# Second-layer attention with four score banks, one projection bank, and odd softmax chunks scaled by POOL

## The chip, the core and the metric

The kernel runs on one core of one Trainium2 chip. The metric is the device time of one execution in microseconds, lower is better; the time before is the median of three runs. A core has five engines that run beside each other and wait for one another by semaphores: PE (TensorE: matmuls and transposes), DVE (VectorE), ACT (ScalarE), POOL (GpSimd) and SP (SyncE, which here only issues DMAs). Matmul results land in PSUM, of which there are eight banks of 128 partitions x 512 f32; PE writes them, ACT and DVE read them, POOL does not touch them here.

## The reference, cut to what matters

The program is a two-layer decoder trunk on 512 tokens of width 1024. Layer 0 is a gated DeltaNet layer, layer 1 a sliding-window attention with grouped heads; each layer also attends with four heads into 256 memory tokens, and each ends with an output projection and a SwiGLU block. The change is in the attention of layer 1:

```python
proj = h @ swa_w_q[bl]                       # 512 x 1024: 768 window queries, 256 memory queries
q = apply_partial_rope(proj[..., :768], cos, sin)
# window attention, 12 heads of 64, per block of 128 queries over 256 keys (previous and own block)
s = einsum(q, k) * (64 ** -0.5); s = where(mask, s, -inf)
m = maximum(max(s), sink)
p = exp(s - m)
p = p / (sum(p) + exp(sink - m))
o = einsum(p, v)
# memory attention, 4 heads of 64, over 256 memory tokens
s = einsum(mem_q, mem_k) * (64 ** -0.5); o = einsum(softmax(s), mem_v)
x = x + concat([mix_out, mem_o]) @ w_out[layer]
x = x + swiglu(rms_norm(x), w_gate_up, w_down)
```

## The kernel before, in words

Activations lie transposed: a tile holds 128 features (partitions) x 512 tokens. Every large product is done in three f32r matmuls per 128x128 weight block (`mm3`: high part by high part, high by low, low by high), so a projection of one 128-feature tile (`project`) is 8 blocks x 3 = 24 matmuls of 128x512 that accumulate in one PSUM bank. The weight of a projection is loaded by SP into `wraw`, its high part made by ACT (`whi`), its low part by DVE (`wlo`).

The attention of layer 1 is `swa`. It has eight query tiles: 0 to 5 are window tiles (two heads each), 6 and 7 memory tiles. `queries(t)` projects one tile; for a window tile `rope` then reads the bank twice on DVE (a stream shuffle, a multiply by `cosT`), multiplies by `sinT` and adds. `score(t)` makes the scores of the four token chunks n = 0 to 3 and both heads b: the PSUM tile `qk` is two banks and holds two chunks, so a tile takes two of them. For window tiles DVE adds the band mask and takes the maximum (one custom instruction and one accumulator read per chunk and head) into `sm` in SBUF; for memory tiles DVE takes the maximum and ACT writes the exponentials. `weigh(t)` then does the rest: ACT takes the exponentials of a window tile, DVE the reciprocal of the sums, each chunk is scaled in place (even n by DVE with `ts`, odd n by ACT with `copy`), PE transposes it into a `pt` bank, the transposed chunk is copied to `pf` (n = 2 by DVE, the others by ACT), and PE multiplies by the values into the bank `sc`, which `split` writes out as the pair `mix[t]` (ACT the high part `h`, DVE the low part `l`).

The eight banks of this stage are named in `build`: two for projections (`pj`), one for small things (`g`), one two-bank `qk` tile, two `pt`, one `sc`. The main loop, for t = 0 to 5, traces `queries(t + 1)`, `score(t)` and then `weigh` of the tile scored two steps earlier; the last two `weigh` follow the loop. `output` projects the eight mixed tiles to x with banks pj, pj, g in turn; it takes the mixed tiles in the order 6, 7, 0 to 5, so that it can begin before the last are there.

The order of the work on each engine is not the order of the text: a scheduler with costs of its own places the traced instructions on each engine ahead of time, and on the chip each engine works its list strictly in that order and stops where a semaphore is missing. PE therefore fills its waits with matmuls of the next projection only where the list has them.

Of the kernel before, what the change touches and what calls it, by code (L numbers as in the profile page):

```python
# [13 lines left out]
ALU = mybir.AluOpType  # L14
# [4 lines left out]
P = 128  # L19
# [4 lines left out]
NC = 4  # L24
# [61 lines left out]
class Builder:  # L86
# [139 lines left out]
    def build(self):  # L226
        tc, nc, a = self.tc, self.nc, self.a
        with ExitStack() as st:
            opened = lambda name, **kw: tc.tile_pool(name=name, bufs=1, reuse_waits="tile", **kw)
            pool = lambda name, **kw: st.enter_context(opened(name, **kw))  # L230
            cp = pool("const")
            self.wpool, self.apool = pool("w"), pool("acta")
            self.dpool = pool("scratch", space=DRAM)
            self.load_constants(cp)
            self.weng = nc.vector
            with opened("layer0", side="right") as self.mpool:
                with self.banks(pj=3, g=2, sc=3):
                    with opened("early", side="right") as ep:
                        self.mem_and_norm(ep)
                        self.gates(ep)  # L240
                    with opened("gdn", side="right") as gp:
                        mix = self.gdn(gp)
                    self.bpool, xp = pool("actb"), pool("x")
                    self.x = [self.t(xp, [P, T], F32, f"x{k}") for k in range(KD)]
                    for k in range(KD):
                        nc.sync.dma_start(self.x[k], a["xT"][:, k, :])
                    self.rstd, self.cosT, self.sinT = (self.t(xp, [P, T], F32, n) for n in ("rstd", "cosT", "sinT"))
                    h = self.output(xp, 0, mix, self.bpool)
            with opened("ffn0", side="right") as fp, self.banks(pj=2, g=6):
                self.ffn(fp, xp, 0, h, self.apool, rope=True)  # L250
            with self.banks(pj=2, g=1, qk=1, pt=2, sc=1):
                with opened("swa", side="right") as sp:
                    mix = self.swa(sp)
                h = self.output(xp, 1, mix, self.apool)
            with opened("ffn1", side="right") as fp, self.banks(pj=2, g=6):
                self.ffn(fp, xp, 1, h, self.bpool)
# [492 lines left out]
        return sm, mx, den, nm  # L749

    def weigh(self, pool, scores, vv, m, out, sinks):

        nc = self.nc
        win = sinks is not None
        own = "pt" in self.pbufs
        half = [slice(0, 64), slice(64, P)]
        sm, mx, den, nm = scores
        if win:
            sk = sinks.unsqueeze(2).to_broadcast([P, 2, NC])
            v4 = lambda ap: ap.rearrange("p (b n) -> p b n", b=2)  # L760
            self.stt(v4(mx), v4(mx), 0.125, sk, ALU.mult, ALU.max)
            self.ts(nm, mx, -1.0, ALU.mult)
            es = self.t(pool, [P, 2 * NC], F32, "es", 2)
            self.tt(nc.vector, v4(es), v4(nm), sk, ALU.add)
            self.fn(es, es, AF.Exp)
            for n in range(NC):
                c0 = 0 if n else P
                for b in range(2):
                    i = b * NC + n
                    self.fn(sm[n][:, b, c0:], sm[n][:, b, c0:], AF.Exp, scale=0.125, bias=nm[:, i:i + 1],  # L770
                            accum_out=den[:, i:i + 1])
            self.tt(nc.vector, den, den, es, ALU.add)
        nc.vector.reciprocal(den, den)
        o = self.bank("sc")
        group = NC if own else 2
        for n in range(NC):
            if n % group == 0:
                pf = {}
            k0 = 1 if win and n == 0 else 0
            p = sm[n][:, :, k0 * P:]  # L780
            dn = den.rearrange("p (b n) -> p n b", b=2)[:, n, :]
            for b in range(2):
                if n % 2:
                    self.copy(p[:, b], p[:, b], scale=dn[:, b:b + 1])
                else:
                    self.ts(p[:, b], p[:, b], dn[:, b:b + 1], ALU.mult)
            pt = self.bank("pt" if own else "g", [P, 2, 2, P])
            for j in range(k0, 2):
                for b in range(2):
                    turned = self.tr(pt[:, j, b, :], sm[n][:, b, j * P:(j + 1) * P])  # L790
                    if self.ahead is not None:

                        self.nosync(turned, self.ahead)
                        self.ahead = None
            pf[n] = self.t(pool, [P, 2, 2, P], F32, "pf", group)
            if own and n == 2:
                nc.vector.tensor_copy(pf[n][:, k0:], pt[:, k0:])
            else:
                self.copy(pf[n][:, k0:], pt[:, k0:])
            if (n + 1) % group:  # L800
                continue
            for n, t in pf.items():
                for j in range(1 if win and n == 0 else 0, 2):
                    for b in range(2):
                        v = vv[n - 1 + j][:, half[b]] if win else vv[j][:, m * P + 64 * b:m * P + 64 * b + 64]
                        ins = self.mm(o[half[b], n * P:(n + 1) * P], v, t[:, j, b, :], win and n == 0 or j == 0, j == 1)
                        if turned is not None:
                            self.nosync(ins, turned)
                            turned = None
        self.split(o, *out)  # L810


    def output(self, xp, layer, mix, hpool):

        nc, a = self.nc, self.a
        self.weng = nc.vector
        h = []
        self.acc = None
        for m in range(KD):
            ps = self.project(a["wout"][layer, m], mix, ("pj", "pj", "g")[m % 3],  # L820
                              (6, 7, 0, 1, 2, 3, 4, 5))
            self.tt(nc.vector, self.x[m], ps, self.x[m], ALU.add)
            hl = self.pair(hpool)
            self.split_gain(self.x[m], self.gain(G_FFN[layer], m), *hl)
            h.append(hl)
            self.acc = self.accumulate(xp, self.acc, self.x[m], m)
        return h
# [189 lines left out]

    def rstd_from(self, acc, t=slice(0, T)):
        self.use(LN_EXP)
        ps = self.bank("g")[:, t]  # L1020
        self.mm(ps, self.ones, acc)
        self.rsqrt(self.rstd[:, t], ps, D)

# [46 lines left out]
    def swa(self, sp):  # L1070
        nc, a = self.nc, self.a
        memK, memV = self.fetch(sp, "mk"), self.fetch(sp, "mv")
        hk, h, qs, mix = [], [], {}, {}
# [5 lines left out]
        kk, vv = [], []  # L1079

        def queries(t):
            ps = self.project(a["wq"][t], h)
            if len(qs) == 0:
                self.rstd_from(self.acc)
                for table in (self.cosT, self.sinT):
                    self.tt(nc.vector, table, table, self.rstd, ALU.mult)
            qs[t] = self.t(sp, [P, T], F32, "q", 3)
            if t < 6:
                self.rope(sp, ps, qs[t])
            else:  # L1090
                self.tt(nc.vector, qs[t], ps, self.rstd, ALU.mult)

        def keys():
            kk.append(self.t(sp, [P, T], F32, "ks"))
            self.rope(sp, self.project(a["wkv"][0], hk), kk[0])

        def values():
            ps = self.project(a["wkv"][1], hk)
# [3 lines left out]

        def transpose_values():
            v = vv.pop()
            pt = self.bank("g")
            for c in range(NC):
                self.tr(pt[:, c * P:(c + 1) * P], v[:, c * P:(c + 1) * P])
            vt = self.t(sp, [P, NC, P], F32, "vt")
            self.copy(vt.rearrange("p c i -> p (c i)"), pt)
            vv.extend(vt[:, c, :] for c in range(NC))  # L1110

        def score(t):
            got[t] = self.scores(sp, qs[t], kk[0] if t < 6 else memK[t - 6], t < 6)

        def weigh(t):
            mix[t] = self.pair(self.bpool)
            if t < 6:
                self.weigh(sp, got[t], vv, t, mix[t], sinks[:, t, :])
            else:
                self.weigh(sp, got[t], memV, t - 6, mix[t], None)  # L1120

        got = {}
        queries(6)
# [4 lines left out]
        transpose_values()  # L1128
        queries(0)
        score(7)  # L1130

        behind = [6, 7]
        for t in range(6):
            if t < 5:
                queries(t + 1)
            score(t)
            behind.append(t)
            weigh(behind.pop(0))
        for t in behind:
            weigh(t)  # L1140
        return [mix[t] for t in range(KD)]

    def final(self, fp, squares, t):
# [85 lines left out]
```

## Time and profile before

| | |
|---|---|
| time, median of 3 runs | 1168.39 us (1166.91 to 1168.46) |
| the profiled execution's own time | 1169.1 us |
| its span, first to last instruction | 1167.3 us |
| mean granted TensorE clock | 0.996 of full speed |
| busy: PE / weight loads / DVE / ACT / POOL | 1144.1 / 999.2 / 834.2 / 629.4 / 82.9 us |
| waits of PE over the whole span, longest first | 6.9, 2.2, 2.1, 1.0, 0.9, 0.9, 0.5, 0.4 us |

A page of the profile shows one execution: busy time by engine, the chain that ended last, and groups of equal instructions. The trace behind it gives every instruction with its start, its length and what ended the idle time before it. Rows of a timeline start with the start in us from the beginning of the span and the length in us; matmuls overlap, so the distance from start to start, not the length, is what one costs PE. In this execution `swa` runs from about 657 to 776 us, and the part from the first scores to the end of the second output projection from 682.4 to 778.1 us.

### The profile page before, as it was taken

Reading aid. Unit: us, or ns where it says so; the run is one execution under the profiler, and the core shown is the slowest. Engines: PE = TensorE matmul, PEld = TensorE weight load, DVE = VectorE, ACT = ScalarE, POOL = GpSimd, SP = SyncE. Lnnn points to the kernel's source line nnn. Section 1 sums busy time; section 2 is a strip of 40 time slices with the busy share of each in tenths; the row PEclk is TensorE's granted clock in tenths of the full one; section 3 lists DMA queues with packets and bytes.
Section 4 is the critical chain, followed back from the end, with each engine's and each line's share of the span. In section 5 each row is a group of like instructions: output and inputs, shape, how many; then the busy total and the mean of one; then the engine's idle time right before and its main releaser. Section 6 shows DMA issues by size and latency. Waiting matters only on the chain.

```text
span 1167.3 us, 19448 instructions
## 1 busy us (share of the span) xinstructions
PE 1144.1 (98%) x7410; PEld 999.2 (86%) x7410; DVE 834.2 (71%) x1558; ACT 629.4 (54%) x1250; POOL 82.9 (7%) x93
## 2 busy tenths in 40 slices
PE   7999999999999999999999999999999999999996
PEld 6888777877889998899998877688999988999986
DVE  6654877767788876488965768758788734889654
ACT  7579564366466642256643546865566422566433
POOL 0210000000011101011100000010011000111000
PEclk9999999999999999999999999999999999999998
DMA  8334352224557735467623421153477633776232
GB/s 306 126 110 113 114 127 92 72 91 162 163 136 187 175 102 155 123 165 180 163 79 99 129 82 55 37 126 110 100 189 183 155 99 106 168 171 172 76 99 84
DMA packets 72944, 151.22 MB, mean 130 GB/s; under 512 B 16732, under 2 KB 19444, under 8 KB 72852
## 3 DMA queue, kind: packets, MB, share of 16 engines
q1 hardware_dynamic: 61908, 130.06, 36.3%
q0 software_dynamic: 10944, 19.93, 10.9%
q8 instruction: 58, 0.95, 0.4%
q14 instruction: 34, 0.28, 0.1%
HBM read 143.00 MB, written 6.96 MB: 128 GB/s over the span
## 4 chain that ended last, share of the span: by engine, by line
PE 91%; ACT 4%; DVE 3%; DMA 1%; issue 0%; SPq 0%; DVEq 0%; ACTq 0%
PE pj L143 44%; PE g L143 39%; PE sc L143 6%; ACT sm L131 1%; PE g L147 1%; PE pt L147 1%; DVE wlo L150 1%; ACT sm L137 1%; DMA wraw<-in_wmk 1%; ACT whi L137 0%; ACT T L137 0%; PE qk L143 0%; DVE mx L743 0%; DVE sm L739 0%; DMA wraw<-in_wdn 0%
## 5 line engine op out<-in xcount | busy, mean ns | idle before, releaser
L137 ACT ACTIVATE whi<-wraw 128x512 fp32r<-128x512 f32 (+3 forms) x325 | 243.1, 754 | 292.3 <-PE pj L143 191.4
L150 DVE TENSOR_TENSOR wlo<-wraw,whi 128x512 fp32r<-128x512 f32 (+3 forms) x325 | 271.9, 845 | 109.0 <-ACT whi L137 103.5
L143 PE MATMUL pj<-h,whi 128*128 128x512 f32 (+1 forms) x676 | 265.9, 394 | 0.2
L143 PE MATMUL pj<-l,whi 128*128 128x512 f32 (+1 forms) x676 | 265.2, 392 | 0.0
L143 PE MATMUL pj<-h,wlo 128*128 128x512 f32 (+1 forms) x676 | 264.4, 392 | 0.0
L143 PE MATMUL g<-T,whi 128*128 128x256 f32 x1216 | 220.5, 282 | 0.0
L143 PEld LDWEIGHTS g<-T,whi 128*128 128x128 f32 x1216 | 187.0, 189 | 1.1 <-DVE fu L153 1.1
L143 PE MATMUL g<-T,wlo 128*128 128x256 f32 x608 | 171.1, 281 | 0.0
L143 PE MATMUL g<-h,whi 128*128 128x256 f32 (+1 forms) x516 | 152.8, 296 | 0.0
L143 PE MATMUL g<-h,wlo 128*128 128x256 f32 (+1 forms) x516 | 152.0, 295 | 0.0
L143 PE MATMUL g<-l,whi 128*128 128x256 f32 (+1 forms) x516 | 151.8, 294 | 0.0
L143 PEld LDWEIGHTS pj<-h,whi 128*128 128x128 f32 x676 | 127.1, 188 | 28.4 <-issue 2.7
L143 PEld LDWEIGHTS pj<-h,wlo 128*128 128x128 f32 x676 | 127.2, 188 | 27.2 <-issue 2.2
L143 PEld LDWEIGHTS pj<-l,whi 128*128 128x128 f32 x676 | 127.2, 188 | 26.3 <-issue 1.2
L143 PEld LDWEIGHTS g<-T,wlo 128*128 128x128 f32 x608 | 114.4, 188 | 0.0
L143 PEld LDWEIGHTS g<-h,whi 128*128 128x128 f32 x516 | 98.0, 190 | 2.9 <-issue 0.2
L143 PEld LDWEIGHTS g<-l,whi 128*128 128x128 f32 x516 | 97.9, 190 | 2.9 <-issue 0.5
L143 PEld LDWEIGHTS g<-h,wlo 128*128 128x128 f32 x516 | 98.0, 190 | 2.4
L978 POOL DMA_DIRECT2D ws<-in_wgu x38 | 33.6, 883 | 735.1 <-DVE wlo L150 335.3
L137 ACT ACTIVATE whi<-ws 128x512 fp32r<-128x512 f32 x76 | 48.0, 631 | 49.3 <-PE g L143 41.2
L150 DVE TENSOR_TENSOR fu<-pj,rstd 128x512 f32<-128x512 f32 (+1 forms) x34 | 22.4, 660 | 53.0 <-PE pj L143 53.0
L150 DVE TENSOR_TENSOR wlo<-ws,whi 128x512 fp32r<-128x512 f32 x76 | 52.1, 686 | 7.3 <-ACT whi L137 7.2
(346 smaller groups left out, 1626.0 us busy)
## 6 DMA issues: line engine op xcount, KB each, us to landing
wraw<-in_wgu SPq DMA_DIRECT2D x50, 512.0 KB, 4.1
ws<-in_wgu SPq DMA_DIRECT2D x76, 256.0 KB, 3.5
ws<-in_wgu POOLq DMA_DIRECT2D x76, 256.0 KB, 4.9
wraw<-in_win SPq DMA_DIRECT2D x26, 512.0 KB, 3.6
wraw<-in_wdn SPq DMA_DIRECT2D x32, 384.0 KB, 3.2
wraw<-in_wdn SPq DMA_DIRECT2D x32, 320.0 KB, 2.9
wraw<-in_wgu SPq DMA_DIRECT2D x38, 256.0 KB, 4.6
wraw<-in_wout SPq DMA_DIRECT2D x16, 512.0 KB, 3.6
```

Of the source, the lines that this page charges most:

```text
L131: ins = self.nc.scalar.activation(out, in_, func, **kw).ins
L137: self.copied = self.nc.scalar.activation(out, in_, AF.Copy, **kw).ins
L143: return self.nc.tensor.matmul(out, lhsT, rhs, start=start, stop=stop, skip_group_check=more).ins
L147: return self.nc.tensor.transpose(out, in_, self.ident[:k, :k]).ins
L150: return eng.tensor_tensor(out=out, in0=a, in1=b, op=op).ins
L978: nc.gpsimd.dma_start(s1, a22, accum_op=ALU.add)
```

## The change

The score tiles get two buffers of two banks (`qk=2`), and the projections one bank (`pj=1`); the bank `g` is gone from this stage. What used `g`, and the projections of query tile 7 and of the keys, use the `pt` banks, which are not needed for transposes yet at that time; the output projection takes pj, pt, pt in turn. `weigh` is cut in two functions, `softmax` (exponentials, reciprocal, all four scalings) and `weighed` (transposes and values), and the loop of `swa` traces `softmax` of a tile right after `weighed` of the one before it, that is one step earlier than before. The odd chunks are scaled by POOL in this stage (`tensor_scalar`), the even ones by DVE as before. `weigh` of layer 0 now calls both functions, so that its four scalings are traced ahead of its transposes; there the odd chunks stay on ACT.

On PE's list the two halves of a tile's scores now follow each other, and a projection is cut in at most three pieces: after the scores and the first transposes one matmul, after the first half of the values one to three, and then the rest.

```diff
-            with self.banks(pj=2, g=1, qk=1, pt=2, sc=1):
+            with self.banks(pj=1, qk=2, pt=2, sc=1):
...
     def weigh(self, pool, scores, vv, m, out, sinks):
+        self.softmax(pool, scores, sinks)
+        self.weighed(pool, scores, vv, m, out, sinks is not None)
+
+    def softmax(self, pool, scores, sinks):
...
         nc.vector.reciprocal(den, den)
+        for n in range(NC):
+            p = sm[n][:, :, P if win and n == 0 else 0:]
+            dn = den.rearrange("p (b n) -> p n b", b=2)[:, n, :]
+            for b in range(2):
+                if n % 2 and "pt" in self.pbufs:
+                    nc.gpsimd.tensor_scalar(out=p[:, b], in0=p[:, b], scalar1=dn[:, b:b + 1], scalar2=None, op0=ALU.mult)
+                elif n % 2:
+                    self.copy(p[:, b], p[:, b], scale=dn[:, b:b + 1])
+                else:
+                    self.ts(p[:, b], p[:, b], dn[:, b:b + 1], ALU.mult)
+
+    def weighed(self, pool, scores, vv, m, out, win):
...
-            for b in range(2):
-                if n % 2:
-                    self.copy(p[:, b], p[:, b], scale=dn[:, b:b + 1])
-                else:
-                    self.ts(p[:, b], p[:, b], dn[:, b:b + 1], ALU.mult)
             pt = self.bank("pt" if own else "g", [P, 2, 2, P])
...
-            ps = self.project(a["wout"][layer, m], mix, ("pj", "pj", "g")[m % 3],
+            ps = self.project(a["wout"][layer, m], mix, ("pj", "pt", "pt")[m % 3] if "pt" in self.pbufs else ("pj", "pj", "g")[m % 3],
...
-        ps = self.bank("g")[:, t]
+        ps = self.bank("pt" if "pt" in self.pbufs else "g")[:, t]
...
-            ps = self.project(a["wq"][t], h)
+            ps = self.project(a["wq"][t], h, "pt" if t > 6 else "pj")
...
-            self.rope(sp, self.project(a["wkv"][0], hk), kk[0])
+            self.rope(sp, self.project(a["wkv"][0], hk, "pt"), kk[0])
...
-            pt = self.bank("g")
+            pt = self.bank("pt")
...
-        def weigh(t):
+        def softmax(t):
+            self.softmax(sp, got[t], sinks[:, t, :] if t < 6 else None)
+
+        def weighed(t):
             mix[t] = self.pair(self.bpool)
...
         score(7)
+        softmax(6)
...
             score(t)
             behind.append(t)
-            weigh(behind.pop(0))
-        for t in behind:
-            weigh(t)
+            weighed(behind.pop(0))
+            softmax(behind[0])
+        weighed(behind[0])
+        softmax(behind[1])
+        weighed(behind[1])
```

More of the change, by code (lines that the diff above doesn't have):

```diff
@@ L751, in weigh @@
     def weigh(self, pool, scores, vv, m, out, sinks):
+        self.softmax(pool, scores, sinks)
+        self.weighed(pool, scores, vv, m, out, sinks is not None)
+    def softmax(self, pool, scores, sinks):
         nc = self.nc
         win = sinks is not None
-        own = "pt" in self.pbufs
-        half = [slice(0, 64), slice(64, P)]
         sm, mx, den, nm = scores
@@ L773, in weigh @@
         nc.vector.reciprocal(den, den)
+        for n in range(NC):
[9 more added lines that the diff above has]
+    def weighed(self, pool, scores, vv, m, out, win):
+        nc = self.nc
+        own = "pt" in self.pbufs
+        half = [slice(0, 64), slice(64, P)]
+        sm = scores[0]
         o = self.bank("sc")
@@ L779, in weigh @@
             k0 = 1 if win and n == 0 else 0
-            p = sm[n][:, :, k0 * P:]
-            dn = den.rearrange("p (b n) -> p n b", b=2)[:, n, :]
-            for b in range(2):
-                if n % 2:
-                    self.copy(p[:, b], p[:, b], scale=dn[:, b:b + 1])
-                else:
-                    self.ts(p[:, b], p[:, b], dn[:, b:b + 1], ALU.mult)
             pt = self.bank("pt" if own else "g", [P, 2, 2, P])
@@ L1113, in score @@
             got[t] = self.scores(sp, qs[t], kk[0] if t < 6 else memK[t - 6], t < 6)
-        def weigh(t):
+        def softmax(t):
+            self.softmax(sp, got[t], sinks[:, t, :] if t < 6 else None)
+        def weighed(t):
             mix[t] = self.pair(self.bpool)
[L1117 to L1120, printed above, removed]
+            self.weighed(sp, got[t], *((vv, t) if t < 6 else (memV, t - 6)), mix[t], t < 6)
         got = {}
```

## The prediction

> **What bounds the kernel now.** I read the page's busy table first, then the windows of the stage that changes, the waits of PE, and the timelines of PE, DVE and ACT.
>
> ```profile
> span 1167.3 us, 19448 instructions
> PE 1144.1 (98%) x7410; PEld 999.2 (86%) x7410; DVE 834.2 (71%) x1558; ACT 629.4 (54%) x1250; POOL 82.9 (7%) x93
> ```
>
> PE is busy 98% of the span, so only what PE waits for, or loses between its pieces, can be won. The profiled execution took 1169.1 us, 1.8 more than its span and 0.7 above the median of 1168.4; I sum in differences and put them on the median. Two windows, from the first scores (T0) to the last query projection's end, and from there to the end of the second output projection:
>
> ```profile
> core 0: us, PE busy (x) PEld busy (x) DVE busy (x) ACT busy (x) POOL busy (x), PEclk, DMA share, GB/s
> 682.30:747.40 65.10, 63.37 (x425) 46.99 (x424) 49.10 (x160) 45.40 (x138) 0.00 (x0) 1.00 0.18 54
> 747.40:778.10 30.70, 29.63 (x249) 23.04 (x249) 18.92 (x72) 22.61 (x70) 1.38 (x2) 1.00 0.23 59
> PE pt L147 <- ACT pf L137: 2.2, 4, 0.7
> PE qk L143 <- ACT sm L131: 0.5, 1, 0.5
> ```
>
> In the main part PE idles 65.10 - 63.37 = 1.7 us, in the tail 1.07. The last two rows (waits of PE from 665 to 790 us) name them: transposes that wait until ACT has copied the bank before, and the second scores of tile 6, which wait for the one `qk` tile. DVE is busy 49 of 65 us: it is the engine next in line, and it works its list in order. Now the prices of PE, from its timeline:
>
> ```profile
> 707.31 0.93 PE L143 MATMUL qk<-ks,q 64*128 64x128 f32 x8
> 708.17 0.50 PE L143 MATMUL pj<-h,wlo 128*128 128x512 f32 x1
> 708.50 0.39 PE L143 MATMUL pj<-h,whi 128*128 128x512 f32 x1
> 708.73 0.39 PE L143 MATMUL pj<-l,whi 128*128 128x512 f32 x1
> ...
> 709.89 0.39 PE L143 MATMUL pj<-h,whi 128*128 128x512 f32 x1
> 710.21 1.13 PE L143 MATMUL qk<-ks,q 64*128 64x256 f32 x8
> 711.28 1.09 PE L147 MATMUL pt<-consts,sm 128*128 128x128 f32 x8
> 712.12 0.47 PE L143 MATMUL pj<-l,whi 128*128 128x512 f32 x1
> 712.62 1.15 PE L147 MATMUL pt<-consts,sm 128*128 128x128 f32 x8
> 713.69 1.97 PE L143 MATMUL sc<-pf,mv 128*64 128x128 f32 x32
> ```
>
> Start to start, a projection matmul costs 0.23 us, but 0.33 as the first of a run (708.17 to 708.50) and 0.32 as the last (709.89 to 710.21): each run of projection matmuls between other work loses about 0.2 us. A window tile's scores cost 0.86 + 1.07 = 1.93, its transposes 0.84 + 1.07, its values at most 1.97 us.
>
> **What the change removes.** The list of the changed program holds the same matmuls. The six query projections come in 14 runs in place of 18 in the main part: -0.8 us. The wait of 0.5 for `qk` goes, for there are now four banks of scores. The 2.2 us behind `pf` divide into 1.1 in the main part and 1.1 in the tail; ACT loses the odd scalings (below) and reaches its copies sooner, so I let the 1.1 go too. That the exponentials are listed a round earlier wins nothing by itself: no row of PE's waits names them. Removed from the main part: 0.8 + 0.5 + 1.1 = 2.4 us.
>
> **What it adds there: one projection bank, and DVE in front of it.** A projection can begin only when rope's shuffle and cos multiply have read the bank, and the second half of a tile's values needs the copy of chunk 2, which DVE does after rope and after all eight maxima. DVE's prices:
>
> ```profile
> 735.43 0.73 DVE L1065 STREAM_SHUFFLE rs<-pj 128x512 f32<-128x512 f32 x1
> 736.05 0.67 DVE L150 TENSOR_TENSOR q<-pj,cosT 128x512 f32<-128x512 f32 x1
> 736.65 0.68 DVE L150 TENSOR_TENSOR rs<-rs,sinT 128x512 f32<-128x512 f32 x1
> 737.24 0.28 DVE L739 CUSTOM_DVE_ANT_0 sm<-qk,consts 128x128 f32<-128x128 f32 x1
> 737.45 0.68 DVE L150 TENSOR_TENSOR q<-q,rs 128x512 f32<-128x512 f32 x1
> 738.06 0.42 DVE L739 CUSTOM_DVE_ANT_0 sm<-qk,consts 128x256 f32<-128x256 f32 x1
> 738.40 0.08 DVE L739 DVE_READ_ACCUMULATOR2_ANT mx<- 128x1 f32 x1
> 695.94 0.88 DVE L157 TENSOR_SCALAR sm<-sm,den 128x256 f32<-128x256 f32 x3
> 740.31 1.22 DVE L150 TENSOR_TENSOR wlo<-wraw,whi 128x1024 fp32r<-128x1024 f32 x1
> L797 DVE COPY pf<-pt 128x512 f32<-128x512 f32 x8 | 5.5, 690 | 3.5 <-PE pt L147 3.5
> ```
>
> From the start of the shuffle to the end of that copy: shuffle, cos, sin 1.81, a short maximum 0.21, the add 0.61, six maxima of 256 at 0.34 and a short one, 2.25, the copy 0.69, together 5.6 us. PE, from the end of the projection to the second half of the values: scores 1.93, first transposes 0.84, one matmul 0.4, the others 1.0, half the values 1.0, one or two fill matmuls and the changes between them 0.6 to 0.8, together 5.75 to 6.0 us. So there is 0.15 to 0.4 us of slack, and whatever DVE comes late to the shuffle beyond it, PE stands still. Is DVE late? Before the loop stand the memory tiles, whose maxima alternate with ACT:
>
> ```profile
> 682.39 1.13 PE L143 MATMUL qk<-mk,q 64*128 64x256 f32 x8
> 684.50 0.68 DVE L743 TENSOR_REDUCE mx<-qk 128x2 f32<-128x512 f32 x1
> 685.22 0.17 DVE L157 TENSOR_SCALAR nm<-mx 128x2 f32<-128x2 f32 x1
> 685.42 0.47 ACT L131 ACTIVATE sm<-qk,nm 128x256 f32<-128x256 f32 x1 [0.68 <-DVE nm L157]
> 686.48 0.69 DVE L743 TENSOR_REDUCE mx<-qk 128x2 f32<-128x512 f32 x1 [1.09 <-ACT sm L131]
> 726.61 0.39 ACT L131 ACTIVATE sm<-sm,nm 128x128 f32<-128x128 f32 x1
> 730.33 0.84 ACT L137 ACTIVATE pf<-pt 128x256 f32<-128x256 f32 x2
> 739.45 1.71 ACT L137 ACTIVATE sm<-sm,den 128x256 f32<-128x256 f32 x4
> ```
>
> The first maximum starts at T0 + 2.2, and from one maximum over its exponentials to the next of the same `qk` are 1.98 us. In the changed list DVE does the maxima of tile 6, its reciprocal and its two scalings all before it shuffles q0. The third and fourth maxima come at T0 + 4.2 and, behind 0.9 for the negation and four exponentials at 0.47 on ACT, at T0 + 6.95; then 0.7 to the negation, 0.2 and two exponentials, 0.2 each for the start of reciprocal and scaling (I take what the negation took after its maximum's end), and two scalings (three in a row took 0.88), 0.55: the shuffle starts at T0 + 9.7. PE ends q0 at T0 + 8.3 (scores 2.1, transposes of v 0.5, 24 matmuls 5.5, changes 0.2). DVE is 1.4 late; the bank is free at 10.9, PE wants it at 10.4: **+0.5**. The next round on DVE, rope 1.81 and add 0.6, four maxima 2.4, a `wlo` 1.14, two scalings 0.5, negations 0.6, the last two exponentials of tile 7 with reciprocal and its scalings 2.2, is 9.2 us: shuffle of q1 at T0 + 18.9, q1's end at T0 + 16.5. Late by 2.4, less 0.3 of slack: **+2.1**, 0.7 of it at the projection bank and the rest at the values. Tile 0's list still has its sum of exponentials ahead of the shuffle of q2: 5.6 + scalings, maximum, `wlo`, negation 2.2, eight exponentials 3.7 (726.61 to 730.33) and some 0.8 of hand-overs and reciprocal, 12.3, against PE's 11.9 with changes and the 2.1 already lost in that round counted once: late by some 0.7: **+0.6**. The shuffle of q3 waits for no exponentials (DVE's list from shuffle to shuffle is 5.6 + 3.2 us): 0. The shuffle of q4 waits for tile 2's and is late by 0.1 to 0.5: **+0.2**. That of q5: 0. Added: 3.4 us. The main part: 3.4 - 2.4 = +1.0.
>
> **POOL and the tail.** ACT's four scalings of a tile (1.71, 0.43 each) go to POOL. No row has this operation; rows of POOL from both sides:
>
> ```profile
> L150 POOL TENSOR_TENSOR DT<-gcr,consts 128x512 f32<-128x512 f32 x6 | 8.5, 1458 | 10.6 <-DMA gcr<-dr 10.6
> L366 POOL MEMSET wabs<- 128x512 f32 x1 | 0.5, 525 | 0.3 <-POOLq L1221 0.3
> L150 POOL TENSOR_TENSOR DT<-gcr,consts x6: 1283/1294/2291, 55.5 to 62.7; 128x512 f32<-128x512 f32 x6
> 57.73 1.36 DVE L150 TENSOR_TENSOR wlo<-wraw,whi 128x1024 fp32r<-128x1024 f32 x1 [0.89 <-ACT whi L137]
> ```
>
> At half the width two inputs cost 0.73 and no input 0.26; one input lies between, and I take 0.5. The Trainium skill ("GPSIMD Engine Reference", Engine selection) calls one-input work on this engine roughly line-rate; with its 1.03 cycles per element (Elementwise) at 1.2 GHz that would be an estimate of 0.22 us and the sum about 0.5 lower, and no run here shows it. In the loop a tile's transposes come a round later, so POOL is covered at either price. In the tail it is not: the scalings of tiles 3, 4 and 5 come straight ahead of their transposes. There the runs fall from 10 to 6 (-0.8), but only one output projection is on the list as filler, where two and the begin of a third were: 17 matmuls are spent before the last softmax. I count waits of 0.3 for the copies of tile 2 behind ACT's exponentials, 0.9 for tile 3 (reciprocal behind a `wlo`, then two POOL operations, then its copies), 0.4 for tile 4 and 0.6 for tile 5, in all 2.2 against 1.07 now: 1.1 - 0.8 = **+0.3**. Layer 0 only has its scalings listed 0.4 earlier than its copies; its neighbours are the same: 0. POOL's DMAs for the next block stand behind the scalings, but their data is wanted after six more output projections, 6 x 24 x 0.23 = 33 us later: 0.
>
> Sum: +1.0 + 0.3 = +1.3, so 1169.7 us (1170.4 for an execution like the profiled one). By its least sure terms, the 2.1 and the 0.6, this case reaches from 1167.2 to 1171.2.
>
> **Rivals.** *DVE is on time, and the banks do what they can.* If the memory tiles' maxima overlap ACT better than I chain them, the 3.4 and the tail's waits vanish: -2.4 - 0.8 - 1.07 = -4.3, 1164.1. For it: DVE is busy only 49 of 65 us, so room exists. Against it: 686.48 shows DVE idle 1.09 us for ACT in just this chain, and in the changed list the shuffle stands behind it. It decides when the shuffle of q1 starts within 0.3 us of q1's end.
>
> *POOL sets the end.* At 0.73 a tile's last odd chunk is ready 2.9 us after the reciprocal, where 0.5 gives 2.0 and ACT gave 1.7; tiles 3, 4 and 5 wait for it in turn: 3 x 0.9 = 2.7 more than my case, 1172.4. It decides from about 0.5 us per scaling on. For it too: one of the six POOL operations took 2.29 us instead of 1.29 around a DVE `wlo`, which took 1.36 instead of 1.22; the engines held each other up, and rope's sin multiply and add and `wlo` have two SBUF inputs like that one, so DVE may also lose 0.1 to 0.5 at each meeting, in the rounds of q1 and q2 where it is late already. The Trainium skill ("SBUF — State Buffer", Who interferes with whom) states that rule: a DVE instruction with two SBUF inputs and a GpSimd instruction that reads SBUF exclude each other for a whole instruction; the two rows agree. Against it: in the loop POOL has a round to spare.
>
> *Half of it.* DVE is late, but by half (1.7 of the 3.4), and the tail keeps its 0.3 less half its waits (1.1): 1169.7 - 1.7 - 1.1 = 1166.9.
>
> **Chances.** My case 0.45, DVE on time 0.17, POOL 0.28, half 0.10. 0.2%, about what a measurement can tell here, is 2.3 us: below 1166.1 faster, above 1170.7 slower. My case lies within it but for 0.07 slower; the half gives 0.03 faster. So faster 0.20, same 0.45, slower 0.35. The range, 1165.5 to 1173.5, holds my case, most of the POOL case and the half, and leaves out most of the first rival.
>
> **What would show it.** Right: PE waits named `pf` from DVE (the copy of chunk 2) and `pj` from DVE (`q`) in the rounds of q1 and q2, 2 us and 0.6 us; none for `qk`; a POOL scaling near 0.5. Wrong: DVE idle for PE before those shuffles (first rival), or PE waits on POOL in the tail of over 2 us (second).

## The result: slower by 0.4%, and the profile after

| | before | after |
|---|---|---|
| median (6 runs each, same chip) | 1168.1 us (1166.8 to 1169.0) | 1172.5 us (1172.0 to 1173.8) |
| ratio after to before, 95% interval | | 1.0040 (1.0027 to 1.0053) |
| profiled execution: time / span | 1169.1 / 1167.3 us | 1172.0 / 1170.2 us |

The forecast of 1169.7 us was 2.8 us too low; the result lies in the range, on its slow side, and above the 1170.7 us from which the prediction speaks of slower: no change had the larger chance there, 0.45 against 0.35. The busy table of the changed kernel, and the windows of its two parts, cut at the same marks of PE's work as before (start of the first scores, end of the last query projection, start of the last matmul of the second output projection). The windows of the kernel before between these marks come last:

```profile
span 1170.2 us, 19511 instructions
PE 1144.9 (98%) x7410; PEld 999.5 (85%) x7410; DVE 835.7 (71%) x1558; ACT 617.2 (53%) x1218; POOL 115.0 (10%) x125
```

```profile
core 0: us, PE busy (x) PEld busy (x) DVE busy (x) ACT busy (x) POOL busy (x), PEclk, DMA share, GB/s
680.30:746.76 66.46, 62.95 (x427) 47.40 (x426) 49.89 (x160) 37.48 (x118) 20.91 (x20) 1.00 0.15 51
746.76:781.52 34.76, 32.08 (x250) 23.75 (x249) 22.58 (x76) 20.29 (x61) 14.77 (x16) 1.00 0.27 77
```

```profile
682.39:747.55 65.16, 63.43 (x427) 47.06 (x426) 49.10 (x160) 45.46 (x139) 0.00 (x0) 1.00 0.17 53
747.55:778.11 30.56, 29.49 (x249) 22.96 (x250) 18.93 (x72) 22.47 (x70) 1.39 (x2) 1.00 0.23 59
```

Column one is the stretch, two its length, three PE's busy time and instructions. The main part grew by 1.3 us, the tail by 4.2, 5.5 in all, at full clock in both kernels. That is inside the interval of the medians (3.2 to 6.2 us). The waits of PE in these two parts, and the group of POOL's new instruction:

```profile
PE sc L143 <- DVE pf L809: 1.5, 2, 1.3
PE pt L147 <- POOL sm L781: 1.5, 4, 0.6
PE pj L143 <- DVE q L150: 1.4, 2, 1.2
PE qk L143 <- DVE mx L739: 0.4, 1, 0.4
PE pt L147 <- ACT pf L137: 0.4, 2, 0.2
PE qk L143 <- ACT sm L131: 0.3, 1, 0.3
```

```profile
L781 POOL TENSOR_SCALAR sm<-sm,den 128x256 f32<-128x256 f32 x32 | 32.2, 1022 | 167.2 <-PE qk L143 116.6 <-DVE nm L157 23.8 <-DVE den L775 11.8
```

One scaling on POOL takes 1.02 us, twice what I took and above my upper bound of 0.73. The waits named POOL are 1.5 us, but the tail lost 4.2; most of the rest stands in no row of waits. It stands in PE's busy time: with the same matmuls it rose in the tail by 2.6 us, from 29.49 to 32.08; idle time rose by 1.6, from 1.07 to 2.68. The timeline of PE shows how; first before, then after, only rows of transposes:

```profile
752.35 0.87 PE L147 MATMUL pt<-consts,sm 128*128 128x128 f32 x6
754.25 1.14 PE L147 MATMUL pt<-consts,sm 128*128 128x128 f32 x8 [0.56 <-ACT pf L137]
761.33 0.87 PE L147 MATMUL pt<-consts,sm 128*128 128x128 f32 x6
```

```profile
755.43 1.13 PE L147 MATMUL pt<-consts,sm 128*128 128x128 f32 x6
757.22 1.20 PE L147 MATMUL pt<-consts,sm 128*128 128x128 f32 x8 [0.19 <-ACT pf L137]
761.44 0.44 PE L147 MATMUL pt<-consts,sm 128*128 128x128 f32 x2 [0.27 <-POOL sm L781]
762.37 0.55 PE L147 MATMUL pt<-consts,sm 128*128 128x128 f32 x3 [0.49 <-POOL sm L781]
763.22 1.50 PE L147 MATMUL pt<-consts,sm 128*128 128x128 f32 x8
770.63 0.98 PE L147 MATMUL pt<-consts,sm 128*128 128x128 f32 x7 [0.60 <-POOL sm L781]
```

Eight transposes in a row took 1.50 us (763.22) and six took 1.13 (755.43), where 0.87 for six and, with their fill, about 1.1 for eight is the price. A transpose is under way for 0.27 us and its successor may start 0.11 behind it; a pause between two of them shows as idle only where it outlasts what is still in the pipe. Added up from the start marks of all rows of the tail, one transpose to the next took 5.39 us before (46 pairs) and 9.64 after (48 pairs). Of these 9.64 us 1.54 are the waits named POOL; about 2.5 of the growth are pauses that no row names, as much as the busy time rose.

### The profile page after: what moved, and what is told of

Its sections match the earlier page's. It is cut to its first block, busy times and chain, and to the rows that moved or that the text cites. A ratio compares the mean times of both kernels' runs of the same rounds, so it can differ in the third digit from the quotient of the medians.

```text
span 1170.2 us, 19511 instructions
## 1 busy us (share of the span) xinstructions
PE 1144.9 (98%) x7410; PEld 999.5 (85%) x7410; DVE 835.7 (71%) x1558; ACT 617.2 (53%) x1218; POOL 115.0 (10%) x125
## 4 chain that ended last, share of the span: by engine, by line
PE 90%; DVE 5%; ACT 3%; issue 1%; DMA 1%; POOL 0%; SPq 0%; DVEq 0%; POOLq 0%; ACTq 0%
PE pj L143 42%; PE g L143 38%; PE sc L143 6%; PE pt L143 3%; ACT sm L131 1%; DVE wlo L150 1%; PE g L147 1%; DVE sm L739 1%; DMA wraw<-in_wmk 1%; DVE mx L743 1%; ACT whi L137 0%; POOL sm L781 0%; PE pt L147 0%; DVE q L150 0%; DVE btmp L150 0%
## 5 line engine op out<-in xcount | busy, mean ns | idle before, releaser
L143 PE MATMUL pj<-h,whi 128*128 128x512 f32 (+1 forms) x636 | 249.7, 393 | 1.5 <-DVE q L150 1.4
L143 PE MATMUL pj<-l,whi 128*128 128x512 f32 (+1 forms) x636 | 249.6, 392 | 0.0
L143 PE MATMUL pj<-h,wlo 128*128 128x512 f32 (+1 forms) x636 | 248.1, 390 | 0.0
L143 PE MATMUL g<-h,whi 128*128 128x256 f32 (+1 forms) x500 | 146.5, 293 | 0.0
L143 PE MATMUL g<-h,wlo 128*128 128x256 f32 (+1 forms) x500 | 145.8, 292 | 0.0
L143 PE MATMUL g<-l,whi 128*128 128x256 f32 (+1 forms) x500 | 145.5, 291 | 0.0
L143 PEld LDWEIGHTS pj<-h,whi 128*128 128x128 f32 x636 | 119.4, 188 | 27.2 <-DVE q L150 2.0
L143 PEld LDWEIGHTS pj<-l,whi 128*128 128x128 f32 x636 | 119.6, 188 | 25.0 <-issue 1.6
L143 PEld LDWEIGHTS pj<-h,wlo 128*128 128x128 f32 x636 | 119.5, 188 | 24.6 <-issue 1.1
L143 PEld LDWEIGHTS g<-h,whi 128*128 128x128 f32 x500 | 95.0, 190 | 2.3 <-PE pj L143 0.2
```

What stands on the lines that cost most here:

```text
L143: return self.nc.tensor.matmul(out, lhsT, rhs, start=start, stop=stop, skip_group_check=more).ins
```

## The experiments

Two theories of the tail. A: POOL's 1.02 us, because the scalings of tiles 3 to 5 come straight ahead of their transposes. B: the lists, because one projection bank leaves PE without filler, that is without matmuls to put between the steps of a tile that depend on each other; B1 makes the banks the cause, B2 the earlier softmax. C, beside them: layer 0, where the changed kernel's profile was ahead by 2.1 us. Stage times below are between the marks named above. Each ratio is to the kernel before on the same chip.

| kernel | median us | ratio, 95% interval | main part | tail |
|---|---|---|---|---|
| before | 1168.0 | | 65.16 | 30.56 |
| after | 1172.5 | 1.0040 (1.0027 to 1.0053) | 66.46 | 34.76 |
| odd_act | 1173.5 | 1.0040 (1.0028 to 1.0052) | 65.62 | 34.15 |
| pool_loop | 1173.1 | 1.0045 (1.0032 to 1.0058) | 66.43 | 34.11 |
| pool_only | 1170.1 | 1.0017 (1.0009 to 1.0026) | 65.93 | 33.18 |
| l0_only | 1168.1 | 0.9999 (0.9990 to 1.0007) | 65.20 | 30.55 |
| split_only | 1167.6 | 0.9995 (0.9986 to 1.0004) | 64.96 | 30.55 |
| banks_only | 1172.0 | 1.0039 (1.0027 to 1.0052) | 65.71 | 33.90 |
| old_banks | 1171.0 | 1.0027 (1.0016 to 1.0038) | 65.78 | 33.18 |
| dve_only | 1167.1 | 0.9995 (0.9986 to 1.0003) | 64.50 | 30.53 |
| pj1_g | 1181.2 | 1.0095 (1.0079 to 1.0110) | 80.89 | 30.57 |
| pj1_pt | 1185.2 | 1.0134 (1.0119 to 1.0149) | 80.79 | 35.30 |
| qk2_pt1 | 1172.5 | 1.0030 (1.0019 to 1.0041) | 65.83 | 32.50 |
| split_dve | 1167.7 | 0.9982 (0.9972 to 0.9993) | 64.37 | 30.41 |

The last four share runs of the kernel before with a median of 1169.4 us; the ratios allow for it, the medians alone do not. The main parts of pj1_g and pj1_pt can't be set against the others: two projections that the other kernels have done before the first scores lie within them (475 matmuls in place of 427, 48 x 0.23 = 11 us).

**POOL taken out of the change (odd_act, pool_loop).** This is what odd_act changes, cut to its effect; in pool_loop it holds for tiles 3, 4 and 5 alone, and POOL keeps the others.

```diff
-                if n % 2 and "pt" in self.pbufs:
-                    nc.gpsimd.tensor_scalar(out=p[:, b], in0=p[:, b], scalar1=dn[:, b:b + 1], scalar2=None, op0=ALU.mult)
-                elif n % 2:
+                if n % 2:
                     self.copy(p[:, b], p[:, b], scale=dn[:, b:b + 1])
```

> The changed kernel, but the odd chunks of the second layer are scaled by ACT again (four ACT instructions of 0.43 us per tile in place of four POOL ones of 1.02); banks, the exponentials listed a round earlier and layer 0 stay as changed. Theory A (POOL's price, twice what I assumed, makes the tail's loss of 4.2 us, because there each tile's scalings stand straight ahead of its transposes): the tail comes back by 3 to 4 us, the main part stays, so about 1169. Theory B (the lists make the loss: one projection bank, DVE late, and only one output projection as filler in the tail): ACT now carries the scalings and the pf copies again, so 1172 to 1174, no better than the changed kernel's 1172.5. No PE wait may name POOL.

> The changed kernel, with POOL scaling the odd chunks of tiles 6, 7, 0, 1 and 2 only, and ACT those of tiles 3, 4 and 5, whose transposes follow in the tail. Theory A: the loss sits in the tail alone, and POOL is covered elsewhere, so 1169 (as with ACT everywhere, within 0.7). Theory B: 1172 to 1173. If POOL also hurts in the main part (it met DVE there: four scalings took 4.3 to 4.7 us in place of 3.7), this one is slower than ACT everywhere by 0.5 to 1.5.

Windows of the tail of odd_act and of pool_loop:

```profile
748.77:782.92 34.15, 31.35 (x248) 23.56 (x249) 21.74 (x76) 24.71 (x73) 3.48 (x4) 1.00 0.32 80
```

```profile
748.10:782.21 34.11, 31.31 (x249) 23.55 (x249) 21.73 (x76) 24.57 (x73) 3.52 (x4) 1.00 0.31 81
```

No POOL scaling is in either stretch (POOL's four instructions there issue DMAs), and the tail is only 0.6 us shorter. Theory A falls: in the changed kernel other waits take over when POOL's are gone (of odd_act's, ACT for `pf` 1.7 us in the stage and for `h` 0.7). In the main part POOL does cost something, 66.5 against 65.6 us, where I had it covered. So odd_act's stage is 1.4 us shorter than that of the change (99.8 against 101.2), but its whole time is no better: a difference of 1.4 us is as large as the half-widths of the two intervals, and in odd_act's profile the clock was halved once ahead of the stage (last section), which cost 1.7.

**POOL put into the kernel before (pool_only).**

```diff
-                if n % 2:
-                    self.copy(p[:, b], p[:, b], scale=dn[:, b:b + 1])
+                if n % 2 and "pt" in self.pbufs:
+                    nc.gpsimd.tensor_scalar(out=p[:, b], in0=p[:, b], scalar1=dn[:, b:b + 1], scalar2=None, op0=ALU.mult)
```

> The kernel before, with one edit: POOL scales the odd chunks of the second layer, at its old place, chunk by chunk ahead of the transposes. Theory A (POOL's price of 1.02 us, 2.04 a chunk against ACT's 0.86): each of 8 tiles has its transposes 1.2 to 2.4 us later; in the loop 0.84 us of the other chunk's transposes and the fill matmuls cover part, in the tail (3 or 4 tiles) little: 1172 to 1177, waits of PE transposes on POOL of 4 to 8 us. Theory B (POOL is covered, the lists and banks make the loss): 1167 to 1168.5, for ACT is free sooner for its copies (2.2 us of waits).

Slower by 2 us, between the two expectations. Its longest waits of PE in the stage:

```profile
PE pt L147 <- POOL sm L784: 0.9, 2, 0.5
PE qk L143 <- ACT sm L131: 0.8, 2, 0.5
PE pt L147 <- ACT pf L137: 0.5, 2, 0.4
```

Here too the named waits on POOL (0.9 us) are less than the stage lost (0.8 + 2.6 us). So POOL is a loss of its own on the old banks, and on the new banks one of 1.4 us (odd_act above): 3.9 for the banks (below) and 3.4 for POOL give 5.5 together, not 7.3.

**Layer 0 alone (l0_only).** Here `scaled` holds the scaling of one chunk as before; layer 0 does all four ahead of its first transpose.

```diff
         nc.vector.reciprocal(den, den)
+        if "pt" not in self.pbufs:
+            for n in range(NC):
+                self.scaled(n, sm, den, win)
```

> The kernel before, with one edit: layer 0 scales all four chunks ahead of its first transpose, as the changed kernel does; the second layer is the kernel before. Theory C (this reordering is worth the 2.1 us by which the changed kernel was ahead before the second layer's attention, by a shorter wait of PE on DVE near 140 us and no fall of the clock to 0.50 behind it): 1166 to 1166.5. Against it (that fall came and went between executions): 1168.1, no change, and the clock falls near 141 us here or not as it happens.

No change; theory C falls. What the two profiles differed by ahead of the stage is told in the last section.

**The two parts of the change alone (split_only, banks_only).** split_only lists softmax a round earlier, as the change does, on the old banks; with ACT's scalings and layer 0 of before. banks_only is the following edit with the order and ACT's scalings of before; what used g, and query tile 7 and the keys, go to pt, and the output projection takes pj, pt, pt, as in the change:

```diff
-            with self.banks(pj=2, g=1, qk=1, pt=2, sc=1):
+            with self.banks(pj=1, qk=2, pt=2, sc=1):
...
```

> The kernel before with one part of the change alone: the exponentials and scalings of a tile are listed a round ahead of its transposes; old banks (two for projections, two for scores), ACT for the odd chunks, old order in layer 0. Theory B1 (the single projection bank makes the loss, through DVE's late rope and a tail without its filler): about 1167 to 1168.5, no loss, since both projection banks are there. Theory B2 (the order makes it: DVE and ACT take a tile's softmax ahead of rope and of the copies of the tile before): 1170 to 1173.

> The kernel before with the new banks alone: four banks of scores, one for projections, and the other users moved to the pt banks; exponentials, scalings and order in place as before, ACT for the odd chunks. Theory B1 (one projection bank): 1171 to 1174, most of the 5.5 us of the kernel with ACT's scalings, with waits named pj from DVE q, and the tail near 34 us in place of 30.6. Theory B2 (the order): 1167 to 1168.5.

The windows of the main part and the tail, first split_only, then banks_only:

```profile
681.99:746.95 64.96, 62.73 (x427) 46.86 (x426) 49.05 (x160) 45.74 (x140) 0.00 (x0) 1.00 0.16 52
746.95:777.49 30.54, 29.47 (x248) 22.97 (x249) 18.91 (x72) 22.18 (x68) 1.72 (x2) 1.00 0.24 61
```

```profile
681.29:747.00 65.71, 63.08 (x427) 47.43 (x426) 48.09 (x160) 45.37 (x138) 0.00 (x0) 1.00 0.16 52
747.00:780.90 33.90, 31.12 (x248) 23.66 (x249) 21.89 (x76) 24.68 (x73) 3.48 (x4) 1.00 0.32 83
```

This settles B1 against B2: the order costs nothing on the old banks, the new banks alone cost 3.9 us of the 5.5, 3.3 of them in the tail, and PE's busy time in the tail rises from 29.5 to 31.1 us with no POOL scaling in it.

**The change with the old banks (old_banks)**: the banks of before, with softmax a round earlier, POOL for the odd chunks and layer 0 as changed.

> The changed kernel with the old banks: exponentials a round earlier and POOL for the odd chunks stay. POOL alone cost the kernel before 2.1 us. If the earlier softmax is what POOL needs as its cover, this one is 1168 to 1169, the main part without loss. If POOL's cost adds to that of the order: 1170 to 1172. Under B1 it must be faster than the changed kernel by at least 2 us, under B2 it is as slow.

Main part 65.78, tail 33.18: as pool_only. So the earlier softmax gives POOL no cover that it hadn't: POOL costs the stage 3.4 us either way (99.1 against 95.7 us in the old order, 99.0 against 95.5 in the new one), and 2.1 and 3.4 us by the medians.

**One bank, and where the second output projection stands (pj1_g, pj1_pt).** The kernel before with one projection bank; this is pj1_g, and pj1_pt has `("pj", "pt", "pt")` for the first of the two triples in the last line and nothing else changed:

```diff
-            with self.banks(pj=2, g=1, qk=1, pt=2, sc=1):
+            with self.banks(pj=1, g=1, qk=1, pt=2, sc=1):
...
-            ps = self.project(a["wout"][layer, m], mix, ("pj", "pj", "g")[m % 3],
+            ps = self.project(a["wout"][layer, m], mix, (("pj", "g", "pt") if "pt" in self.pbufs else ("pj", "pj", "g"))[m % 3],
```

> The kernel before with one projection bank in place of two (the other stands empty), and the second output projection in the free bank g, so that its list keeps both output projections as filler in the tail. If the tail's loss of 3.3 us comes from the missing filler, it is gone here and the tail is 30.5 to 31; the main part shows what one bank costs in the loop, 0.5 to 1 by the kernels with new banks: in all 1168 to 1169. If one bank for the query projections itself makes the loss, 1170 or more.

> The same with one line different: the second output projection goes to a pt bank, as in the changed kernel, so it can start only behind the last transposes and the first one is the only filler. The two score banks of before stay. Filler theory: the tail is 33 to 34, the time 1171 to 1172, though only the place of one projection differs. Otherwise as the run with g. If the four score banks were part of the loss, this one is below the 1172.0 of the kernel with new banks by over 1.

Both totals were far off. Of the tails, pj1_g's is as the filler theory has it; pj1_pt's goes the way it says and is longer than the 33 to 34 expected. Windows of the tail, pj1_g and pj1_pt:

```profile
760.68:791.25 30.57, 29.75 (x249) 22.98 (x249) 18.92 (x72) 22.36 (x69) 1.35 (x2) 1.00 0.23 62
```

```profile
760.73:796.03 35.30, 31.61 (x248) 23.16 (x249) 22.14 (x76) 24.43 (x71) 3.45 (x4) 1.00 0.33 78
```

With the second output projection in a bank that is free (g), the tail is that of the kernel before to 0.01 us, one projection bank or not; with it in a transposition bank, which comes free only behind the last transposes, it is 4.7 us longer, with the score banks of before. PE's list tells why: ahead of the last tile's values pj1_g has 38 matmuls of output projections in the tail and pj1_pt 21; the kernel before has 38, the changed kernel 18. In this pair the place of one projection is the only difference, so it is the cause of the 4.7 us, 2.9 of them idle time and 1.9 busy time of PE. That it is the cause in the changed kernel too follows from its list and from banks_only; the same word changed in the changed kernel itself is not shown, for it has no eighth bank to spare. Why pj1_pt's tail is 1.4 us longer than that of banks_only (33.90), which has the same places for the projections but four score banks, stays open. What I had not expected is the loss ahead of the tail, nearly all of pj1_g's 0.95% (11 us):

```profile
665.37 1.02 PE L143 MATMUL g<-sqa,consts 128*128 128x512 f32 x2
671.27 0.80 PE L143 MATMUL pj<-h,whi 128*128 128x512 f32 x1 [4.88 <-DVE q L150]
```

(timeline of PE in pj1_g). The second projection of the stage cannot begin until DVE has read the first out of its only bank, 4.88 us of standing still, and the clock falls behind it. In all PE waits 9.2 us for that bank behind DVE's `q` in pj1_g, 1.4 in the changed kernel, which has query tile 7 and the keys in the pt banks. Without that move one bank would have cost more: pj1_pt is slower by 1.34%, banks_only by 0.39. These two differ in the score banks as well, so no run gives the price of the move alone.

**Four score banks with both projection banks kept (qk2_pt1).** What used g goes to pt, and the output projection takes pj, pj, pt.

```diff
-            with self.banks(pj=2, g=1, qk=1, pt=2, sc=1):
+            with self.banks(pj=2, qk=2, pt=1, sc=1):
```

> The kernel before with four score banks as in the change, but paid for with the bank g and one of the two transposition banks, so that both projection banks and both output projections as filler stay. Filler theory: the tail holds below 32; what the four score banks bring is at most the 0.5 us of the wait for qk, and one transposition bank adds waits for pf, 8 tiles by some 0.3 us: 1168 to 1171. If four score banks are a gain worth having, under 1167.5.

Slower by 0.3%; the transposes now wait for the copies out of the single pt bank, 3.0 us for DVE's and 2.1 for ACT's, the tail is 1.9 us longer (32.5, where below 32 was expected), and a wait of 1.5 us on DVE stands behind it. In no version did four score banks pay on balance: what they could win was the one wait of 0.5 us for qk, and PE still waits for qk with them, 1.4 us here and 0.7 in the changed kernel (0.3 on ACT and 0.4 on DVE).

**DVE in place of ACT (dve_only, split_dve).**

```diff
-                if n % 2:
-                    self.copy(p[:, b], p[:, b], scale=dn[:, b:b + 1])
+                if n % 2 and "pt" in self.pbufs:
+                    nc.vector.tensor_scalar(out=p[:, b], in0=p[:, b], scalar1=dn[:, b:b + 1], scalar2=None, op0=ALU.mult)
```

> The kernel before with one edit: DVE scales the odd chunks too (0.29 us each in the rows of the even chunks, ACT took 0.43, POOL 1.02). If the 2.2 us of waits for ACT's pf copies come from ACT's scalings standing ahead of them, they shrink to under 1 and the time is 1166.5 to 1167.5; DVE, busy 49 of 65 us, gets 1.2 us a tile more, and if that delays rope or the maxima, waits named DVE take their place: 1168 to 1170.

> Old banks, the earlier softmax, and DVE for the odd chunks: the parts that did no harm alone (1167.6 and 1167.1 against 1168.0). ACT loses 32 scalings of 0.43 us, DVE gets 32 of 0.29, and its scalings are done a round ahead. If the two gains are separate (the waits for pf, and 0.2 of the order), 1166.5 to 1167; if the order puts DVE's scalings in front of rope, 1167.5 to 1169.

The windows of split_dve, main part and tail:

```profile
681.18:745.55 64.37, 63.05 (x427) 46.91 (x426) 53.27 (x179) 34.37 (x108) 0.00 (x0) 1.00 0.17 53
745.55:775.96 30.41, 30.00 (x249) 23.02 (x249) 21.84 (x84) 20.96 (x68) 0.86 (x1) 1.00 0.20 48
```

One scaling lasts 0.35 us on DVE, 0.50 on ACT and 1.02 on POOL. In a row those of DVE and ACT overlap: three took 0.88 us on DVE and four 1.71 on ACT, four on POOL 3.62 to 4.73. dve_only is 0.7 us shorter in the stage; its time alone isn't told apart from no change. With the earlier softmax the stage is 0.9 shorter and the time 0.18% below the kernel before (0.07 to 0.28%): the best version here, and ahead of both kernels, of the first by little. It keeps the change's order and leaves out its banks and POOL.

## Why the prediction was right or wrong, point by point

**Main part, +1.0 forecast, +1.3 measured: the mechanism was right, its sizes partly.** The waits of PE there, and the end of the projection of q1 (timeline):

```profile
691.54 0.50 PE L143 MATMUL pj<-h,whi 128*128 128x512 f32 x1 [1.19 <-DVE q L150]
696.92 0.39 PE L143 MATMUL pj<-h,wlo 128*128 128x512 f32 x1
697.62 2.04 PE L143 MATMUL qk<-ks,q 64*128 64x128 f32 x16 [0.31 <-ACT sm L131]
700.87 0.50 PE L143 MATMUL pj<-h,whi 128*128 128x512 f32 x1 [0.17 <-DVE q L150]
705.23 1.09 PE L143 MATMUL sc<-pf,mv 128*64 128x128 f32 x16 [1.30 <-DVE pf L809]
```

Behind q0 the forecast was 0.5 and the row 1.19; in the round of q1 2.1, split 0.7 and 1.4, against 0.17 and 1.30; q2's 0.6 is 0.2, q4's 0.2 is nothing. In sum 2.9, against 3.4, and 3.2 with the 0.31 for qk: the prediction had the wait for qk gone, and it is not. Idle time in the main part rose by 1.8 us (from 1.73 to 3.51), as the sum has it (3.4 - 0.5 - 1.1). DVE is late for the reason given; its timeline shows it standing behind ACT's last exponentials ahead of the shuffle:

```profile
698.51 0.20 DVE L775 RECIPROCAL den<-den 128x8 f32<-128x8 f32 x1 [1.16 <-ACT sm L131]
698.75 0.84 DVE L157 TENSOR_SCALAR sm<-sm,den 128x256 f32<-128x256 f32 x2
699.51 0.01 DVE L1077 LOAD_MASK_SELECT rs<-pj  x1
699.51 0.73 DVE L1077 STREAM_SHUFFLE rs<-pj 128x512 f32<-128x512 f32 x1
```

The shuffles of q0 and q1 began 9.9 and 19.2 us behind the first scores, where the prediction has 9.7 and 18.9. The shuffle of q1 came 2.2 us behind the end of its projection (699.51 against 697.31), which ends the first rival, DVE on time. In odd_act, without POOL, it came 18.8 us behind the first scores, so DVE is late without POOL too. The credit of 0.8 for fewer runs of projection matmuls was too large: between the marks the trace has 15 runs before and 14 after, where the prediction counted 18, and PE's busy time fell by 0.5 us. And the step that had POOL covered in the loop was wrong by 0.8 us (pool_only against before, the change against odd_act). Without POOL, in odd_act, the main part lost 0.5 us. So that +1.0 came so near +1.3 is partly luck: POOL's 0.8 us, which the sum had at nothing, made up for waits that were put too high.

**Tail, +0.3 forecast, +4.2 measured: here the forecast failed.** The step that failed is "waits of ... in all 2.2 against 1.07 now: 1.1 - 0.8". The waits named in the rows are 2.3 us in sum, as forecast, but not by tile: tile 3 has 0.19 in place of 0.9, tile 4 0.76 in place of 0.4, tile 5 0.95 in place of 0.6, and 0.41 are for qk. I saw that only one output projection was left as filler, counted its 17 matmuls (18 in the trace), and then priced the loss by rows of waits alone, with a credit of 0.8 for the fewer runs. Fewer runs there meant less filler: the runs that went, 4 of 10, had stood between dependent steps. What this cost stood mostly in PE's busy time, which rose by 2.6 us. pj1_g and pj1_pt put the filler's place alone at 4.7 us on the old score banks.

**POOL: the price wrong, the rival's number right and its mechanism not.** I took 0.5 us within 0.26 and 0.73; it is 1.02. The one-input row that I lacked does not lie between a memset and half a two-input multiply. The rival's 1172.4 is the measured time almost exactly, but the tails of odd_act and pool_loop, without POOL in them, are only 0.6 us shorter. That the number fits is luck. By the rival's own sign the waits on POOL had to be over 2 us and are 1.5. The Trainium skill ("GPSIMD Engine Reference", Engine selection) calls one-input work roughly line-rate, from which the estimate was 0.22 us; the trace differs by almost a factor of five, and the measurement decides. The Trainium skill ("SBUF — State Buffer", Who interferes with whom) has a DVE instruction with two SBUF inputs contend with a GpSimd instruction that reads SBUF. The trace agrees in two rows: rope's sin multiply and its add took 0.85 and 0.77 us while POOL scaled, and 0.68 each without. DVE's own scalings, with one input, were held up as well: the two ahead of the shuffle of q1 took 0.84 us beside POOL and 0.62 in odd_act. That pair, and one like it ahead of the shuffle of q0, add up to the 0.45 us by which q1's shuffle came later than in odd_act.

**Layer 0 at zero, POOL's DMAs at zero**: l0_only shows the first; nothing behind the tail moved by more than 0.3 us (from the tail's mark to the last matmul 380.99 before, 380.81 after) for the second. **Half of it** did not happen as a sum, for the main part lost what was forecast; but it did so with POOL's 0.8 us.

## What to carry to other kernels

A bank, buffer or queue place that only lets a later, independent piece of work start early can have a price of which rows of waits name only a part: ask of each bank that a change takes away which filler on PE's list it held, and count the filler between dependent steps, not only the waits. Compare busy time for the same instructions as well as idle time; short pauses hide in a pipelined engine's busy time. And when a rival gives the right number, remove its cause before believing it: without POOL the tail of the changed kernel keeps 3.6 of its 4.2 us.

## What the runs showed of the hardware that was not expected

POOL needs 1.02 us to multiply 128x256 f32 in SBUF by one scalar per partition, DVE 0.35 and ACT 0.50 for the same.

The granted clock halves for stretches of 3.4 us, which cost 1.7 us each, in some executions of a kernel and not in others: the mean clock of the kernel before lay between 0.994 and 0.998. Windows of the kernel before:

```profile
136.00:140.80 4.80, 2.74 (x13) 1.87 (x11) 4.73 (x17) 4.77 (x16) 0.00 (x0) 1.00 0.16 65
140.80:144.20 3.40, 3.40 (x15) 2.46 (x16) 3.07 (x10) 2.76 (x7) 0.00 (x0) 0.50 0.00 0
```

In this profile PE had just waited 2.1 us; the profile of split_only has the same fall at the same place behind a wait of 1.8, that of l0_only has a wait of 1.9 and none. This is most of the 2.1 us by which the changed kernel's profile was ahead in layer 0, and why one profile's span can't be set against another's without looking at the clock. In pj1_g the wait of 4.88 us was followed by 6.8 us at half clock:

```profile
664.00:670.50 6.50, 2.39 (x9) 1.32 (x7) 4.80 (x6) 2.35 (x4) 0.00 (x0) 1.00 0.55 166
670.50:677.30 6.80, 6.03 (x14) 4.78 (x15) 0.71 (x2) 0.00 (x0) 0.00 (x0) 0.50 0.21 73
```

The Trainium skill ("TensorE: Matmul & The Clock Gate", Part 1) describes a gate that halves the clock after an idle window of about 3.4 us and says that its phase varies from run to run; the lengths of 3.4 and 6.8 us agree. On the cause the trace differs: the fall at 140.8 us came behind a wait of 2.1 us only, and in odd_act the clock fell for 3.4 us at 199.9 us, where PE had been busy 4.90 of the 4.90 us ahead of it.
